# Four experts of a block beside each other in the matmul array's column quarters, and expert weights loaded as 8 KB runs per partition

## The chip, the cores and the metric

The kernel runs on one core of one Trainium2 chip. The metric is the device time of one execution in microseconds (us). The kernel before was timed three times: 866.16, 867.60 and 868.55 us, median 867.6. A separate profiled execution gives the views that are quoted below.

The engines are named as in the profile: PE is TensorE (matmuls; PEld is its load of the stationary operand), DVE is VectorE, ACT is ScalarE, POOL is GpSimd, SP is the sync engine, which here only issues transfers (SPq in the rows). DMA is the core's 16 transfer engines together.

## The reference, cut to what matters

One layer of a decoder for 256 tokens of width 1024, all in float32. A first half (normalisation, one wide input projection, a convolution branch and an attention branch, an output projection) yields a new residual `x`. The second half is a mixture of experts:

```python
h2 = rms_norm(x, norm2_g) * (1 + sc2) + sh2            # sc2, sh2: columns of c_act @ w_ada + b_ada
scores = sigmoid(h2 @ w_router)                         # 64 experts; 8 chosen per token, gates gc
g, u = split(einsum('td,edf->tef', h2, w_gu), 2)        # w_gu   (64, 1024, 512): gate and up
routed = einsum('tef,efd->td', silu(g) * u * gc, w_down) # w_down (64, 256, 1024)
out = x + g2 * (routed + shared(h2))
```

Every expert's 1024x512 gate-up matrix (2 MB) and 256x1024 down matrix (1 MB) has to be read once: 192 MB in units of 2^20 bytes, out of some 271 million bytes that the profiled execution moves.

## The kernel before, in words

**Blocks.** After routing, the kernel sorts the experts by their number of tokens and gathers the tokens of a few experts into a block of 128 rows. A block has one of four kinds: H (one expert, 128 rows), M (two experts, 96 and 32 rows), P (two experts, 64 rows each), Q (four experts, 32 rows each). There are 28 blocks: three P blocks whose experts are fixed beforehand, and then `PAT = "QPQQPQPPPMPHPMMMHPMPMPQPP"`. Numbered from 0, the Q blocks are 3, 5, 6, 8 and 25; blocks 0, 1, 2, 4, 7, 9 and so on are P; block 27, the last, is P.

**One block on PE.** `gather` picks token rows by matmuls with a 0/1 matrix (L1532) into `xt`, which holds features on partitions. `experts` then multiplies (L1785): for each of the 8 slices `k` of 128 features, and each expert of the block, the block's rows of that expert are the stationary operand and 128x512 weights stream past; the result is in one PSUM bank, each expert in its rows. The rows of an expert are also the columns of the matmul array that its product uses, so products of different experts with different rows can run beside each other. M has four such tiles of 32 rows (three of them belong to one expert), P has two of 64. `tail` applies the gate (`gate_up`: ACT L1603, DVE L1609), transposes (L1613), copies (ACT L1617), multiplies by the down weights (L1676, 2 slices `f` of features and 2 halves `h` of the output), scales (DVE L1688), splits into two parts (ACT L1745, DVE L1747), and scatters back to the tokens (PE L1699, DVE L1703).

**Parts of a Q block.** `parts("Q")` cuts the four tiles of a Q block into two pairs. The whole of gate-up is done for the first pair of experts, and then for the second pair; the down product likewise. So two of the four column quarters are in use at a time. For every other kind, `parts` is one part with all tiles.

**Weights.** All weights come through one queue that SP issues (`dma`, L269). One transfer is 1 MB: half a gate-up matrix (`("g", j, q)`, four slices of 128 features) or a whole down matrix (`("d", j, 0)`). Each goes to a slot of 8 KB per partition; a slot is free again when PE has done the last product from it (`done`), and only then does SP issue the transfer that is next in `order`. Slice `k` is features `128k` to `128k+127`, one feature per partition (`"(k p) n -> p k n"`): a partition's 8 KB in the slot are four rows of the gate-up matrix (2 KB each) or two rows of the down matrix (4 KB each), from places that are far from each other in memory.

**What sets the order of work.** The kernel is written as generators that yield costs (`yield "P", 0.87`). A planner (`Plan`) runs them at build time with estimated costs and arrival times of transfers, and thereby fixes the order of the instructions on each engine and of the transfers. At run time each engine goes through its instructions in that order and waits where it must. A different cost or a different structure anywhere gives another order, also far from the edit.

**Other places that the change touches.** `ada(i)` for i = 6 to 9 makes `sh2` and `sc2`: a product with `w_ada`, four transposes to turn the row into columns (L762), a sum over four partial results (L767), and one or two small DVE instructions. `turn` scales `x` into `xn2` (ACT L1243 or DVE L1245) and transposes it to `h2T`; the router's weights `wr` and the shared expert use the same layout of features.

Of the kernel before, what the change touches and what calls it, by code (L numbers as in the profile page):

```python
# [38 lines left out]
class Event:  # L39
    t = None  # L40
# [159 lines left out]
def tile_hybrid_block(ctx, tc, x, c, positions, w_ada, b_ada, norm1_g, w_in, conv_dw, conv_dw_b,  # L200
# [70 lines left out]
    def vec(a, n):  # L271
        return a[0].rearrange("(k p) -> k p", p=n)
# [19 lines left out]
    params += [(rbias, bcast(router_bias, NE)), (wr, w_router[0].rearrange("(k p) n -> p k n", p=P))]  # L292
# [45 lines left out]
    def parts(kd):  # L338
        ts = tiles_of[kd]
        return [ts[0:2], ts[2:4]] if kd == "Q" else [ts]  # L340

    for b, (kd, js) in enumerate(blocks):
        gs = []
        for ts in parts(kd):
            es = sorted({t[0] for t in ts})
            gs += [("g", js[e], q) for q in range(2) for e in es]
        ds = [("d", j, 0) for j in js]
        if b == len(blocks) - 1:
            ds = [("d", j, 0, cs) for cs in ENDS for j in js]
            gs = [("g", j, q, c_) for q in range(2) for c_ in range(2) for j in js]  # L350
        order += gs + ds
# [37 lines left out]
    def load(kind, i, q, cut, now):  # L389
# [19 lines left out]
        wsrc = wsrc.rearrange("(k p) n -> p k n", p=P)  # L409
# [107 lines left out]
    pcol = cst.tile([P, 96], F32, name="pcol")  # L517
    ss = cst.tile([P, 8], F32, name="ss")
# [15 lines left out]
    nc.gpsimd.dma_start(rawb[33:49], b_ada[0, 3 * D:5 * D].rearrange("(k p) -> k p", p=P))  # L534
    nc.scalar.dma_start(rawb[49:57], vec(norm2_g, P))
# [94 lines left out]
    def late_columns():  # L630
# [3 lines left out]
        nc.tensor.transpose(p[:, 0:57], rawb[0:57], ident[0:57, 0:57])  # L634
        yield AP(57)
        nc.scalar.copy(pcol[:, 32:89], p[:, 0:57])
# [92 lines left out]
    p2 = cst.tile([P, 2, K], F32, name="p2")  # L729
# [6 lines left out]
    def ada(i, pool):  # L736
# [22 lines left out]
        else:  # L759
            yield "P", 0.43  # L760
            for j in range(4):
                nc.tensor.transpose(p[:, j * P:(j + 1) * P], s[:, j * P:(j + 1) * P], ident)  # L762
            yield pl.ev("cols")
            j = 4 * (i - 6)
            o = p2.rearrange("p a k -> p (a k)")[:, j:j + 4]
            yield TS(4)
            nc.vector.tensor_reduce(o, p.rearrange("p (j g r) -> p j g r", j=4, g=4)[:, :, :, 0], axis=AX.X, op=OP.add)  # L767
            yield TS(4)
            nc.vector.tensor_tensor(o, o, pcol[:, 65 + j:69 + j], op=OP.add)
            jj = slice(j % 8, j % 8 + 4)  # L770
            yield TS(4)
            if i < 8:
                nc.vector.tensor_copy(b2c[:, jj], p2[:, 0, jj])
            else:
                nc.vector.scalar_tensor_tensor(a2c[:, jj], p2[:, 1, jj], 1.0, pcol[:, 81:89][:, jj], op0=OP.add,
                                               op1=OP.mult)
# [462 lines left out]
    def turn(t, q):  # L1239
        d = slice(q * 512, (q + 1) * 512)  # L1240
        e = yield [TS(512), AS(512)]
        if e == "A":
            nc.scalar.activation(xn2[:, t, d], x_sb[:, t, d], AF.Copy, scale=rs2[:, t, 3:4])  # L1243
        else:
            nc.vector.tensor_scalar(xn2[:, t, d], x_sb[:, t, d], rs2[:, t, 3:4], None, op0=OP.mult)  # L1245
# [354 lines left out]
    def gate_up(pg, gate, put=None):  # L1600
# [11 lines left out]
        for f in range(2):  # L1612
            nc.tensor.transpose(pg[:, f * P:(f + 1) * P], act[:, f * P:(f + 1) * P], ident)  # L1613
# [42 lines left out]
    def tail(b, pg):  # L1656
# [10 lines left out]
        for ts in parts(kd):  # L1667
            es = sorted({t[0] for t in ts})
            for e in es:
                yield pl.ev("L", "d", js[e], 0)  # L1670
                yield max(loaded["d", js[e]].at)
            for f in range(2):
                for h in range(2):
                    yield "P", 0.87
                    for e, o, m in ts:
                        nc.tensor.matmul(pd[h][o:o + m], aT[:, f, o:o + m],  # L1676
                                         loaded["d", js[e]].k[f][:, h * 512:(h + 1) * 512],
                                         start=(f == 0), stop=(f == 1))
            for e in es:
                done(("d", js[e]), 0)  # L1680
# [90 lines left out]
    def experts():  # L1771
        for b, (kd, js) in enumerate(blocks):
# [3 lines left out]
            for ts in parts(kd):  # L1776
                es = sorted({t[0] for t in ts})
                for k in range(K):
                    yield pl.ev("xt", b - b % 2, k // 2)
                    for e in es:  # L1780
                        yield pl.ev("L", "g", js[e], k // 2)
                        yield loaded["g", js[e]].at[k]
                    yield "P", 0.87
                    for e, o, m in ts:
                        nc.tensor.matmul(pg[o:o + m], info.xt[:, k, o:o + m], loaded["g", js[e]].k[k],  # L1785
                                         start=(k == 0), stop=(k == K - 1))
                    if b < 2 and k % 4 == 1:
                        for e in es:
                            if loaded["g", js[e]].off[k // 4] != LAST:
                                advance(pl.cur.ready, loaded["g", js[e]].off[k // 4])  # L1790
                    if k % 4 == 3:
                        for e in es:
                            done(("g", js[e]), k // 4)
# [147 lines left out]
```

## Time and profile before

| | |
|---|---|
| profiled execution, its own time | 866.95 us |
| its span, first to last instruction | 865.2 us |
| runs, median (lowest, highest) | 867.6 us (866.16, 868.55) |
| PE busy | 809.2 us, 94% |
| DVE, ACT, POOL busy | 464.9, 311.2, 191.6 us |
| transfers over the span | 271.03 MB, mean 313 GB/s |
| granted TensorE clock, mean | 0.982 |

Time and span are of the same execution; 1.75 us of the time lie outside the span. The first product of block 0 starts at 337 us, so about 528 of the 865 us belong to the experts. A window row of the profile gives, for a stretch of the span, the busy time of each engine with the number of its instructions in brackets, the granted clock (1.00 is full speed), the mean busy share of the 16 transfer engines (it can exceed 1 a little, where packets overlap) and the rate. A timeline row gives start, duration, engine, line, operation, operands and count. PE is counted as busy while any matmul is in flight.

### The profile page before, as it was taken

Reading aid. Unit: us, or ns where it says so; the run is one execution under the profiler, and the core shown is the slowest. Engines: PE = TensorE matmul, PEld = TensorE weight load, DVE = VectorE, ACT = ScalarE, POOL = GpSimd, SP = SyncE. Lnnn points to the kernel's source line nnn. Section 1 sums busy time; section 2 is a strip of 40 time slices with the busy share of each in tenths; the row PEclk is TensorE's granted clock in tenths of the full one; section 3 lists DMA queues with packets and bytes.
Section 4 is the critical chain, followed back from the end, with each engine's and each line's share of the span. In section 5 each row is a group of like instructions: output and inputs, shape, how many; then the busy total and the mean of one; then the engine's idle time right before and its main releaser. Section 6 shows DMA issues by size and latency. Waiting matters only on the chain.

```text
span 865.2 us, 13140 instructions
## 1 busy us (share of the span) xinstructions
PE 809.2 (94%) x4731; PEld 455.6 (53%) x4731; DVE 464.9 (54%) x1083; ACT 311.2 (36%) x682; POOL 191.6 (22%) x242
## 2 busy tenths in 40 slices
PE   3999999999858999999999999999999999999997
PEld 2897766798738776535342433434344343444233
DVE  6559999999975874206242343253433534433333
ACT  4457758667656542203020321212122121232010
POOL 3004899887514740001000000000000000000000
PEclk9999999999967999999999999999999999999999
DMA  9998678558446554999999999999999999979981
GB/s 322 366 340 288 209 253 299 184 207 273 162 152 240 187 197 176 354 389 393 355 394 397 392 397 393 392 397 393 394 392 395 374 341 362 355 278 388 398 303 50
DMA packets 127339, 271.03 MB, mean 313 GB/s; under 512 B 7085, under 2 KB 16901, under 8 KB 127272
## 3 DMA queue, kind: packets, MB, share of 16 engines
q1 hardware_dynamic: 126936, 270.00, 85.2%
q8 instruction: 37, 0.61, 0.3%
q14 instruction: 30, 0.25, 0.1%
q0 software_dynamic: 272, 0.16, 0.1%
q10 hardware_dynamic: 64, 0.02, 0.0%
HBM read 269.11 MB, written 1.05 MB: 312 GB/s over the span
## 4 chain that ended last, share of the span: by engine, by line


## 5 line engine op out<-in xcount | busy, mean ns | idle before, releaser
L1785 PE MATMUL bank<-fa 128*32 128x512 f32 (+2 forms) x1048 | 228.0, 596 | 0.1
L1703 DVE TENSOR_TENSOR fa<-fa,bank 128x512 f32<-128x512 f32 x108 | 73.3, 685 | 108.7 <-PE bank L1699 108.7
L1785 PEld LDWEIGHTS bank<-fa 128*32 128x32 f32 (+2 forms) x1048 | 63.5, 122 | 123.6 <-issue 119.2
L873 DVE SCALAR_TENSOR_TENSOR bank<-fa,tap,bank 128x256 f32<-128x256 f32 x232 | 112.9, 486 | 5.6
L1676 PE MATMUL bank<-fa 128*32 128x512 f32 (+2 forms) x496 | 111.5, 602 | 4.3 <-ACT fa L1617 4.2
L1745 ACT CAST obs<-fa 128x512 fp32r<-128x512 f32 x54 | 33.3, 619 | 150.6 <-DVE fa L1688 139.3
L1699 PE MATMUL bank<-obs,ra 128*128 128x512 f32 x216 | 78.1, 450 | 1.8 <-ACT obs L1745 0.6
L786 POOL TENSOR_TENSOR rb<-fa,rb 128x512 fp32r<-128x512 f32 x44 | 58.6, 1338 | 71.1 <-ACT rb L805 66.9
L1499 ACT ACTIVATE fa<-bank,b2c,a2c 128x256 f32<-128x256 f32 x108 | 53.2, 562 | 44.2 <-PE bank L1532 44.1
L786 POOL TENSOR_TENSOR ra<-fa,ra 128x512 fp32r<-128x512 f32 x48 | 63.9, 1339 | 21.2 <-ACT ra L805 20.6
L1699 PEld LDWEIGHTS bank<-obs,ra 128*128 128x128 f32 x216 | 33.5, 188 | 61.5 <-issue 49.7
L1532 PEld LDWEIGHTS bank<-ra 128*128 128x128 f32 x448 | 55.3, 191 | 12.3 <-issue 4.6
L1603 ACT ACTIVATE h<-bank 128x256 f32<-128x256 f32 x30 | 11.5, 383 | 135.1 <-PE bank L1785 131.1
L1532 PE MATMUL bank<-ra 128*128 128x256 f32 x448 | 59.7, 288 | 0.2 <-ACT fa L1499 0.2
L1785 PE MATMUL bank<-late_w,fa 128*64 128x512 f32 (+1 forms) x168 | 58.1, 596 | 0.0
L805 ACT CAST ra<-fa 128x512 fp32r<-128x512 f32 x76 | 46.7, 623 | 28.7 <-PE bank L822 16.3
L1609 DVE SCALAR_TENSOR_TENSOR fa<-bank,gsc,h 128x256 f32<-128x256 f32 x28 | 13.4, 482 | 75.2 <-ACT h L1603 75.2
L805 ACT CAST rb<-fa 128x512 fp32r<-128x512 f32 x68 | 42.3, 627 | 31.4 <-PE bank L822 21.8
L1676 PEld LDWEIGHTS bank<-fa 128*32 128x32 f32 (+2 forms) x496 | 26.1, 122 | 50.9 <-issue 39.7
L821 PE MATMUL bank<-ra 128*128 128x256 f32 x160 | 48.5, 303 | 3.3 <-ACT ra L1162 1.8
L1688 DVE TENSOR_TENSOR fa<-bank,fa 128x512 f32<-128x512 f32 x54 | 37.0, 686 | 25.5 <-PE bank L1676 25.5
L822 PE MATMUL bank<-ra 128*128 128x256 f32 x160 | 47.1, 295 | 0.9 <-DVE ra L1164 0.8
(380 smaller groups left out, 1375.4 us busy)
## 6 DMA issues: line engine op xcount, KB each, us to landing
fa<-in_w_exp_gu_dram SPq DMA_DIRECT2D x100, 1024.0 KB, 12.5
fa<-in_w_exp_down_dram SPq DMA_DIRECT2D x50, 1024.0 KB, 12.8
fa<-in_w_ada_dram SPq DMA_DIRECT2D x24, 1024.0 KB, 8.0
fa<-in_w_in_dram SPq DMA_DIRECT2D x22, 1024.0 KB, 7.2
late_w<-in_w_exp_gu_dram SPq DMA_DIRECT2D x19, 1024.0 KB, 14.3
late_w<-in_w_exp_down_dram SPq DMA_DIRECT2D x10, 1024.0 KB, 9.8
fa<-in_w_exp_gu_dram SPq DMA_DIRECT2D x18, 512.0 KB, 10.0
fa<-in_w_in_dram SPq DMA_DIRECT2D x12, 512.0 KB, 8.7
```

The lines of the kernel that those rows point to most:

```text
L786: (nc.gpsimd if e == "G" else nc.vector).tensor_tensor(hl[:, 1], w.k[k], hl[:, 0].bitcast(F32), op=OP.subtract)
L805: nc.scalar.copy(hl[:, 0], w.k[k])
L821: nc.tensor.matmul(o, hl[:, 0, mm], src_t[:, k, 0], start=(k == 0 and m % 2 == 0), stop=False)
L822: nc.tensor.matmul(o, hl[:, 0, mm], src_t[:, k, 1], start=False, stop=False)
L873: nc.vector.scalar_tensor_tensor(cv[:, m] if j == TAPS - 1 else acc, u_sb[:, m, j:j + T], tap[:, m, j:j + 1], acc, op0=OP.mult, op1=OP.add)
L1499: nc.scalar.activation(xt[:, k, 0:ns], p3[:, f2, 0:ns], AF.Identity, bias=b2c[:, k:k + 1], scale=a2c[:, k:k + 1])
L1532: nc.tensor.matmul(p3[:, f2, 0:ns], xr[:, a, t, (f + f2) * P:(f + f2 + 1) * P], pm_[:, t, 0:ns], start=(f2 + t + a == 0), stop=(f2 + t + a ...
L1676: nc.tensor.matmul(pd[h][o:o + m], aT[:, f, o:o + m], loaded["d", js[e]].k[f][:, h * 512:(h + 1) * 512], start=(f == 0), stop=(f == 1))
L1688: nc.vector.tensor_tensor(o32, pd[h], g2b[:, h * 512:(h + 1) * 512], op=OP.mult)
L1699: nc.tensor.matmul(p, info.pT[:, t * P:(t + 1) * P], obs[h][a], start=(a == 0), stop=(a == 1))
L1703: nc.vector.tensor_tensor(x_sb[:, t, d], x_sb[:, t, d], p, op=OP.add)
L1785: nc.tensor.matmul(pg[o:o + m], info.xt[:, k, o:o + m], loaded["g", js[e]].k[k], start=(k == 0), stop=(k == K - 1))
```

## The change

Three things are done.

1. `parts` is gone: the products of a Q block run over all four experts for each slice `k` (gate-up) and for each `f`, `h` (down). The weights of a Q block are loaded in the order: first halves of the four gate-up matrices, second halves, four down matrices. The number of matmuls stays the same.
2. A partition now takes neighbouring features: the expert and shared matrices are read with `"(p k) n -> p k n"`, so slice `k` is features `8p + k` (gate-up) or `2p + k` (down), and the 8 KB that a partition takes in one transfer are one run in memory. For the pieces of the last block's gate-up matrices it is 4 KB; for the column pieces of its down matrices the runs stay as they were.
3. Everything that meets those features is permuted to fit: `turn` reads `x` with a stride of eight elements, the transposes after the gate read `act` with a stride of two, the router's weights are read with the new layout, and `ada(6..9)` makes its columns by eight matmuls with one output column each (stationary operand: every eighth column of the row, 64 of them) in place of four transposes and a sum. The planner's cost of that step is 1.0 in place of 0.43. The biases and `norm2_g` for it are now loaded column-wise, both on POOL's queue, in runs of 32 bytes.

```diff
-    def parts(kd):
-        ts = tiles_of[kd]
-        return [ts[0:2], ts[2:4]] if kd == "Q" else [ts]
-
     for b, (kd, js) in enumerate(blocks):
-        gs = []
-        for ts in parts(kd):
-            es = sorted({t[0] for t in ts})
-            gs += [("g", js[e], q) for q in range(2) for e in es]
+        gs = [("g", j, q) for q in range(2) for j in js]
         ds = [("d", j, 0) for j in js]
...
-        wsrc = wsrc.rearrange("(k p) n -> p k n", p=P)
+        wsrc = wsrc.rearrange("(p k) n -> p k n" if kind in ("g", "d", "sg", "sd") else "(k p) n -> p k n", p=P)
...
-    nc.gpsimd.dma_start(rawb[33:49], b_ada[0, 3 * D:5 * D].rearrange("(k p) -> k p", p=P))
-    nc.scalar.dma_start(rawb[49:57], vec(norm2_g, P))
+    nc.gpsimd.dma_start(c2[:, 0:2], b_ada[0, 3 * D:5 * D].rearrange("(a p k) -> p a k", a=2, k=K))
+    nc.gpsimd.dma_start(c2[:, 2], norm2_g[0].rearrange("(p k) -> p k", k=K))
...
-            yield "P", 0.43
-            for j in range(4):
-                nc.tensor.transpose(p[:, j * P:(j + 1) * P], s[:, j * P:(j + 1) * P], ident)
+            h = slice(64 * (i % 2), 64 * (i % 2) + 64)
+            sv = s.rearrange("p (c k) -> p k c", k=K)
+            yield "P", 1.0
+            for k in range(K):
+                nc.tensor.matmul(p[h, k:k + 1], sv[:, k], sel4[:, 0:1], start=True, stop=True)
...
+        o = xn2[:, t, d].rearrange("p (k c) -> p k c", k=4)
+        xk = x_sb[:, t].rearrange("p (c k) -> p k c", k=K)[:, 4 * q:4 * q + 4]
...
-            nc.vector.tensor_scalar(xn2[:, t, d], x_sb[:, t, d], rs2[:, t, 3:4], None, op0=OP.mult)
+            nc.vector.tensor_scalar(o, xk, rs2[:, t, 3:4], None, op0=OP.mult)
...
-            nc.tensor.transpose(pg[:, f * P:(f + 1) * P], act[:, f * P:(f + 1) * P], ident)
+            nc.tensor.transpose(pg[:, f * P:(f + 1) * P], act.rearrange("s (c f) -> s f c", f=2)[:, f], ident)
...
-        for ts in parts(kd):
-            es = sorted({t[0] for t in ts})
-            for e in es:
-                yield pl.ev("L", "d", js[e], 0)
-                yield max(loaded["d", js[e]].at)
-            for f in range(2):
-                for h in range(2):
-                    yield "P", 0.87
-                    for e, o, m in ts:
+        for j in js:
+            yield pl.ev("L", "d", j, 0)
+            yield max(loaded["d", j].at)
+        for f in range(2):
+            for h in range(2):
+                yield "P", 0.87
+                for e, o, m in tiles_of[kd]:
...
-            for ts in parts(kd):
-                es = sorted({t[0] for t in ts})
-                for k in range(K):
-                    yield pl.ev("xt", b - b % 2, k // 2)
-                    for e in es:
-                        yield pl.ev("L", "g", js[e], k // 2)
-                        yield loaded["g", js[e]].at[k]
-                    yield "P", 0.87
-                    for e, o, m in ts:
+            for k in range(K):
+                yield pl.ev("xt", b - b % 2, k // 2)
+                for j in js:
+                    yield pl.ev("L", "g", j, k // 2)
+                    yield loaded["g", j].at[k]
+                yield "P", 0.87
+                for e, o, m in tiles_of[kd]:
```

How this moves instructions is seen on PE in block 25, the last Q block. The rows are line, operation, operands, size of the output and how many follow each other; L1785 is gate-up, L1699 the scatter of an earlier block, L1578 and L1581 small products for a later block. Before, gate-up of the first pair is the two rows with x8, that of the second pair the row with x16:

```order
L1785 MATMUL bank_79<-fa 32x512 x8
L1578 MATMUL bank_74<-ra 128x4 x2
L1581 LDWEIGHTS permb
L1581 MATMUL bank_74<-rtb,permb 64x256
L1581 LDWEIGHTS permb
L1581 MATMUL bank_74<-rtb,permb 64x256
L1699 MATMUL bank_78<-obs,ra 128x512 x2
L1699 MATMUL bank_80<-obs,ra 128x512 x2
L1785 MATMUL bank_79<-fa 32x512 x8
L1699 MATMUL bank_77<-obs,ra 128x512 x2
L1699 MATMUL bank_76<-obs,ra 128x512 x2
L1785 MATMUL bank_79<-fa 32x512 x16
```

In the changed kernel (gate-up is its L1773, the scatter L1689) the same 32 matmuls stand in groups of four, one per expert, which is seen where one of the four experts' weights lie in another buffer (`late_w`):

```order
L1773 MATMUL bank_80<-fa 32x512 x16
L1689 MATMUL bank_78<-obs,ra 128x512 x2
L1773 MATMUL bank_80<-fa 32x512 x2
L1773 MATMUL bank_80<-late_w,fa 32x512
L1773 MATMUL bank_80<-fa 32x512 x3
L1773 MATMUL bank_80<-late_w,fa 32x512
L1773 MATMUL bank_80<-fa 32x512 x3
L1773 MATMUL bank_80<-late_w,fa 32x512
L1773 MATMUL bank_80<-fa 32x512 x3
L1773 MATMUL bank_80<-late_w,fa 32x512
L1773 MATMUL bank_80<-fa 32x512
L1605 MATMUL bank_80<-ident,fa 128x128 x2
```

What moved: the first 16 matmuls (slices 0 to 3) now need the first halves of all four experts, and the next 16 the second halves.

On SP, at the same block's transfers (`TENSOR_LOAD` reads the number of the next expert), the queue before takes two experts' first and second halves, and then the next expert:

```order
L398 TENSOR_LOAD ids
L398 ISA x2
L269 ISA
L269 DMA fa<-in_w_exp_gu_dram 128x4x512
L269 ISA
L269 DMA fa<-in_w_exp_gu_dram 128x4x512
L269 ISA
L269 DMA fa<-in_w_exp_gu_dram 128x4x512
L398 TENSOR_LOAD ids
L398 ISA x2
L269 ISA
L269 DMA fa<-in_w_exp_gu_dram 128x4x512
```

and in the changed kernel first halves of expert after expert:

```order
L391 TENSOR_LOAD ids
L391 ISA x2
L269 ISA
L269 DMA fa<-in_w_exp_gu_dram 128x2048
L391 TENSOR_LOAD ids
L391 ISA x2
L269 ISA
L269 DMA fa<-in_w_exp_gu_dram 128x2048
L391 TENSOR_LOAD ids
L391 ISA x2
L269 ISA
L269 DMA fa<-in_w_exp_gu_dram 128x2048
```

What moved: the order of halves, and the form of a transfer, 128 runs of 2048 floats in place of 128 times four runs of 512. The number of transfers and their bytes are the same. In the first half of the program the order of attention and projection work on PE is also another one from the first changed `ada` step on, because the planner was given another cost there.

More of the change, by code (lines that the diff above doesn't have):

```diff
@@ L633, in late_columns @@
         yield "P", 0.1
-        nc.tensor.transpose(p[:, 0:57], rawb[0:57], ident[0:57, 0:57])
-        yield AP(57)
-        nc.scalar.copy(pcol[:, 32:89], p[:, 0:57])
+        nc.tensor.transpose(p[:, 0:33], rawb[0:33], ident[0:33, 0:33])
+        yield AP(33)
+        nc.scalar.copy(pcol[:, 32:65], p[:, 0:33])
         yield "P", 0.3
@@ L726, in angles @@
         pl.set("lam")
-    p2 = cst.tile([P, 2, K], F32, name="p2")
+    p2 = cst.tile([P, K], F32, name="p2")
     a2c = cst.tile([P, K], F32, name="a2c")
@@ L1666, in tail @@
         pd = yield Get("bank", 2)
[L1667 to L1680 removed]
+        for j in js:
[5 more added lines that the diff above has]
+                for e, o, m in tiles_of[kd]:
+                    nc.tensor.matmul(pd[h][o:o + m], aT[:, f, o:o + m],
+                                     loaded["d", js[e]].k[f][:, h * 512:(h + 1) * 512],
+                                     start=(f == 0), stop=(f == 1))
+        for j in js:
+            done(("d", j), 0)
         pl.put("aT", aT)
@@ L1775, in experts @@
             pg = yield Get("bank")
-            for ts in parts(kd):
-                es = sorted({t[0] for t in ts})
-                for k in range(K):
-                    yield pl.ev("xt", b - b % 2, k // 2)
-                    for e in es:
-                        yield pl.ev("L", "g", js[e], k // 2)
-                        yield loaded["g", js[e]].at[k]
-                    yield "P", 0.87
-                    for e, o, m in ts:
[L1785 to L1793, printed above, removed]
+            for k in range(K):
+                yield pl.ev("xt", b - b % 2, k // 2)
+                for j in js:
+                    yield pl.ev("L", "g", j, k // 2)
+                    yield loaded["g", j].at[k]
+                yield "P", 0.87
+                for e, o, m in tiles_of[kd]:
+                    nc.tensor.matmul(pg[o:o + m], info.xt[:, k, o:o + m], loaded["g", js[e]].k[k],
+                                     start=(k == 0), stop=(k == K - 1))
+                if b < 2 and k % 4 == 1:
+                    for j in js:
+                        if loaded["g", j].off[k // 4] != LAST:
+                            advance(pl.cur.ready, loaded["g", j].off[k // 4])
+                if k % 4 == 3:
+                    for j in js:
+                        done(("g", j), k // 4)
             info.users[0] -= 1
@@ L1905, in tile_hybrid_block @@
                 for f in range(2):
-                    nc.tensor.transpose(B[2 + t][:, f * P:(f + 1) * P], act[:, f * P:(f + 1) * P], ident)
+                    nc.tensor.transpose(B[2 + t][:, f * P:(f + 1) * P], act.rearrange("s (c f) -> s f c", f=2)[:, f],
+                                        ident)
                 nc.scalar.copy(aT.rearrange("p f s -> p (f s)"), B[2 + t][:, 0:T])
```

23 lines of the change are left out of this document (9 added, 14 removed).

## Prediction

> **What bounds the kernel now.** I read the page's slices first, then windows over the five stretches of the expert stage, then PE's and SP's timelines for where a block starts and when its weights are asked for.
>
> ```profile
> PE   3999999999858999999999999999999999999997
> DMA  9998678558446554999999999999999999979981
> 337.00:377.10 40.10, 39.86 (x202) 18.56 (x201) 7.52 (x24) 9.48 (x20) 0.00 (x0) 1.00 0.87 317
> 377.10:538.90 161.80, 158.75 (x788) 62.63 (x787) 57.96 (x131) 30.88 (x65) 5.55 (x4) 1.00 1.03 390
> 538.90:804.30 265.40, 258.21 (x1496) 109.63 (x1495) 104.69 (x230) 61.72 (x127) 0.00 (x0) 1.00 1.00 372
> 804.30:828.50 24.20, 22.71 (x111) 6.83 (x110) 7.19 (x14) 1.90 (x4) 0.00 (x0) 1.00 1.04 393
> ```
>
> From 337 us on, PE is in flight 97 to 99% of the time (the first number after each length), and the transfer engines are full as well (share 1.03, 390 GB/s, between 377.1 and 538.9). Both look like the bound. Which one is it? The next rows are the starts of blocks 3, 9, 25 and 27 on PE and issues on SP.
>
> ```profile
> 372.12 0.99 SPq L269 DMA_DIRECT2D fa<-in_w_exp_gu_dram  x2
> 375.55 6.17 SPq L269 DMA_DIRECT2D fa<-in_w_exp_down_dram  x4
> 377.10 2.34 PE L1785 MATMUL bank<-fa 128*32 128x512 f32 x10
> 477.00 21.45 SPq L269 DMA_DIRECT2D fa<-in_w_exp_gu_dram  x8
> 509.13 1.05 PE L1785 MATMUL bank<-fa 128*32 128x512 f32 x4
> 538.92 0.64 PE L1785 MATMUL bank<-late_w,fa 128*64 128x512 f32 x1
> 804.30 1.05 PE L1785 MATMUL bank<-fa 128*32 128x512 f32 x4
> 842.27 3.60 PE L1785 MATMUL bank<-fa 128*64 128x512 f32 x16
> 852.83 0.64 PE L1718 MATMUL bank<-fa 128*64 128x512 f32 x1
> fa<-in_w_exp_gu_dram SPq DMA_DIRECT2D x100, 1024.0 KB, 12.5
> ```
>
> Block 8, a Q block, starts at 509.1 us. Its eight gate-up transfers are issued from 477.00 to 498.45 and land 12.5 us after issue in the median, so each is there well before PE comes to it. PE never waits for weights; a transfer waits for a slot that PE has to empty. PE sets the pace, and the queue has nothing in reserve: with PE faster, it is next.
>
> **Part 1, the Q blocks on PE.** Gate-up in windows around blocks 5 (Q), 7 (P), 12 (M) and 25 (Q); the first number after the length is PE's busy time in L1785 alone. Then one down product of a P block.
>
> ```profile
> 420.50:456.50 36.00, 14.43 (x64) 3.64 (x66) 1.00 1.04 394
> 493.80:509.10 15.30, 7.28 (x32) 2.09 (x32) 1.00 1.05 387
> 589.00:605.40 16.40, 7.28 (x64) 1.87 (x65) 1.00 1.04 394
> 804.30:828.50 24.20, 14.31 (x64) 3.46 (x64) 1.00 1.04 393
> 838.78 3.65 PE L1676 MATMUL bank<-fa 128*64 128x512 f32 x16
> ```
>
> The M row is what a Q block will be: 64 records of 32 columns in 7.28 us, four tiles side by side, as fast as the 32 records of a P block. A Q block's 64 records take 14.3 to 14.4 now. The change therefore saves 7.1 us of gate-up per Q block, and in the down product one of two passes of 3.65 us: 10.8 us a block, 54 us for five. M streams one matrix three times where Q streams four, but each matmul is a record with its own stream, so I take M's row for Q.
>
> The Trainium skill, "TensorE: Matmul & The Clock Gate", section "Measured speedup vs the span model", speaks against this: three column tiles gave 2.38 times there, not 3. By it a pass of four would take 7.28/0.79 = 9.2 us, and the sum would be some 3 us higher, for block 25 alone, since the others end in a wait for weights anyway. The trace's M row does not show that loss.
>
> **Part 2, the transfers.** The rate of the queue by the run length, in stretches with one kind of weights: 1 KB runs (`w_ada` pieces at the start), 4 KB (down, twice), 2 KB (gate-up, twice). The last two numbers are the busy share and GB/s.
>
> ```profile
> 5.20:10.80 5.60, 0.00 (x0) 0.00 (x0) 4.18 (x40) 1.81 (x5) 1.00 (x2) 1.00 1.06 355
> 380.00:389.80 9.80, 9.80 (x58) 2.85 (x54) 0.00 (x0) 0.00 (x0) 0.00 (x0) 1.00 1.02 411
> 507.20:517.20 10.00, 10.00 (x56) 4.75 (x56) 4.34 (x10) 4.17 (x8) 0.00 (x0) 1.00 1.04 405
> 493.50:506.90 13.40, 13.03 (x58) 4.15 (x59) 5.21 (x10) 1.99 (x4) 0.00 (x0) 1.00 1.05 387
> 565.80:576.00 10.20, 10.20 (x44) 3.37 (x43) 5.18 (x11) 1.57 (x3) 0.00 (x0) 1.00 1.04 391
> ```
>
> A transfer of 2^20 bytes takes 1.0486 MB over the rate: 2.95 us at 1 KB, 2.70 at 2 KB, 2.55 to 2.59 at 4 KB. Each doubling saves about half of what the last did, 0.25 and then 0.13. No row has 8 KB; one more halving gives 2.50. Bounds: 2.57, if 4 KB is already as good as it gets, and 2.42, if the next step saved as much as the last. I take 2.49.
>
> **The sum.** First the blocks from 3 to 8 (Q P Q Q P Q). PE needs 161.8 - 4 x 10.8 = 118.6 us for them. The rate of 411 from 380.0 on is that of block 3's down matrices, so its gate-up weights were in by about 380; earlier transfers wait for slots that blocks 0 to 2 empty, which the change leaves alone, so I take 378. From there to the first halves of block 9 there are 4 + 6 + 12 + 12 + 6 + 12 + 2 = 54 transfers, 54 x 2.49 = 134.5 us, the end at 512.5. That is later than PE would be (377.1 + 118.6 = 495.7), so weights set the pace here, and PE waits 17 us. Block 9 starts at 512.5 in place of 538.9: **-26.4 us**. Slots do not hold the queue back there: a Q block's products now empty four slots at a time in a quarter of the time that the queue needs to fill them.
>
> Blocks 9 to 24 hold eight P, six M and two H: 90 transfers, 224 us, against 265.4 us of PE that the change does not touch. PE sets the pace again, the lead grows, the gain is kept. Block 25 is a Q block with the lead restored: **-10.8**. After it come 12 transfers (30 us) beside 842.3 - 804.3 - 10.8 = 27 us of PE; the queue is some 10 us ahead in the rows above, which covers it: **+0.5**.
>
> The first half pays for the layout.
>
> ```profile
> L762 PE MATMUL bank<-ident,fa 128*128 128x128 f32 x16 | 2.5, 276 | 0.8 <-ACT fa L748 0.8
> L1578 PE MATMUL bank<-ra 128*128 128x4 f32 x42 | 7.6, 250 | 0.0
> 111.00:178.00 67.00, 62.79 (x360) 1.00 0.72 252
> L1245 DVE TENSOR_SCALAR fa<-fa,rs 128x512 f32<-128x512 f32 x2 | 1.0, 477 | 0.7 <-POOL rs L1235 0.7
> L1613 PE MATMUL bank<-ident,fa 128*128 128x128 f32 x60 | 12.3, 289 | 5.8 <-DVE fa L1609 5.8
> L1703 DVE TENSOR_TENSOR fa<-fa,bank 128x512 f32<-128x512 f32 x108 | 73.3, 685 | 108.7 <-PE bank L1699 108.7
> ```
>
> `ada(6..9)`: 16 transposes (2.5 us) go, 32 matmuls with one column come, at 7.6/42 = 0.18 us each by the nearest row (four columns) 5.8 us: +3.3 on PE, which is 94% busy there and has other work to put beside a wait; I take half, +1.6. The two strided DVE scalings of `turn` may rise from 0.48 to the 0.69 us of a DVE instruction on 512 elements with two inputs: +0.4, on the chain to the router. The strided `act` transposes, the router's layout and the two small loads on POOL's queue I put at nothing: the first are as many instructions as before, the others end long before use; were the strided transposes half again as slow, 60 of 0.29 us would cost 4 us in part. **+2.0**, with 0 and 8 as the ends.
>
> Together 865.2 - 26.4 - 10.8 + 0.5 + 2.0 = 830.5 us of span, with the 1.75 outside it 832.2, against 866.95 of this execution. The median of the runs is 0.65 higher, so 832.9: I say **832**. With 2.42 and 2.57 the first term is -30 and -22; with the first half's ends the likeliest case spans 824 to 842.
>
> **Rivals.**
>
> *Long runs gain nothing.* If the rate is set by bytes and not by runs, 54 transfers take 54 x 2.66 = 143.6 us, block 9 starts at 521.6, and the time is 841. Against it: the three rising rates above. Chance 0.12.
>
> *The weights do not bind, PE's saving comes in full.* Then 54 + 3 us less the 2.5 paid: 815. It needs 54 transfers in 118 us, 2.2 each, 480 GB/s, which no row comes near, or an earlier start of the queue. 0.06.
>
> *The clock drops where PE now waits.* The rows: windows with PE's busy time and the granted clock.
>
> ```profile
> 238.60:242.00 3.40, 1.91 (x10) 1.00 1.05 393
> 242.00:245.50 3.50, 1.69 (x6) 0.66 1.05 387
> 295.00:300.00 5.00, 3.83 (x16) 1.00 0.64 211
> 300.00:305.00 5.00, 3.53 (x16) 1.00 0.58 210
> ```
>
> At about half busy the clock fell, at 70 to 77% it stayed. PE would be busy 118.6 of 134.5 us, 88%, but in bursts with gaps of up to 6 us between a block's halves. If a third of the work ran at half clock, PE would need 158 us there, and the gain of blocks 3 to 8 shrinks from 26 to 4: about 854. A few slow bursts only use up PE's own waiting. The skill's page "TensorE: Matmul & The Clock Gate", section "HAM oscillation — how this bites in real kernels", describes just such bursts that start cold after each wait for a transfer; the rows agree that waiting lowers the clock. 0.09.
>
> *The new order of the first half costs.* The planner's changed cost moves attention and projections; 5 to 15 us lost there give 837 to 847 (and as much could be won). 0.07.
>
> *Slower than before.* Reading 8 KB at a time, the 16 engines take places 64 KB apart and each fills one partition for long; if they then meet in the same memory or port, the queue slows. After block 3's gate-up there are 166 transfers, and from the last block's down product to the end are 865.2 - 852.8 = 12.4 us: the time is worse than before from (865.2 - 12.4 - 378)/166 = 2.86 us a transfer on, 367 GB/s, below all but the 1 KB row. 0.04.
>
> *The four tiles do not overlap,* no gain on PE: 867 to 870. The M row is against it. 0.01.
>
> **How the numbers follow.** The forecast's case has 0.61. 820 to 848 holds it, the first rival, and most of the order's and the clock's cases, and leaves about 2 in 10 out. A measurement of this kernel tells a difference of 0.3%, 2.6 us, from none; the runs above spread by that. Faster by more: 0.93; the slow side of the clock's and the order's cases and the missing overlap leave 0.02 within it; slower 0.05.
>
> **What would show it.** Right: L1785 in a Q block 7.3 us; the rate between blocks 3 and 8 about 421 GB/s, with PE waiting for transfers some 17 us there and hardly at all after block 11; block 9 near 512 plus what the first half shifted; block 25 13 us long. Wrong: a rate at or below 411 (the second part fails), PE busy without gaps between 380 and 510 (weights do not bind), a granted clock under 1 there, or block 0 not starting within 335 to 342.

## The result, and the profile after

The changed kernel takes 841.04 us (median of four runs, 838.2 to 842.8), the kernel before, run on the same chip, 867.88 us. The ratio is 0.969, with a 95% interval of 0.966 to 0.972: about 27 us, where 35 were forecast. The profiled execution took 842.05 us, its span is 840.3 us.

First the page's slices of the changed kernel, one digit for each of 40 equal stretches of 21 us; the last row is in GB/s.

```profile
PE   3999999899987999999998988999999999999897
PEclk9999999699997999999999999999999999999999
DMA  9998666545564684799999999999999989969792
GB/s 314 364 361 289 241 226 241 200 158 195 200 213 157 207 324 164 285 348 423 422 418 422 421 421 420 421 421 420 422 420 422 417 328 383 340 269 422 296 404 82
```

From the nineteenth slice (378 us) on, the queue runs at 417 to 423 GB/s for fourteen slices without a dent, and after that with dents: there it waits for slots. PE has its dents ("8") where the queue has none. Next the windows of the changed kernel over the stages that the prediction used (length, then PE, PEld, DVE, ACT, POOL busy, granted clock, share, GB/s). Block 0 starts at 339.0 us, block 3 at 379.2, block 9 at 516.7, block 25 at 789.0, block 26 at 803.0.

```profile
339.00:379.20 40.20, 39.95 (x205) 18.70 (x206) 7.56 (x24) 9.52 (x20) 0.00 (x0) 1.00 0.86 322
379.20:516.70 137.50, 127.82 (x787) 58.90 (x786) 55.84 (x128) 30.16 (x63) 5.56 (x4) 0.98 1.01 421
516.70:789.00 272.30, 264.08 (x1511) 114.48 (x1513) 110.76 (x241) 64.01 (x130) 0.00 (x0) 1.00 0.96 390
789.00:803.00 14.00, 12.44 (x101) 3.44 (x100) 2.91 (x5) 0.76 (x2) 0.00 (x0) 0.96 0.72 283
803.00:840.30 37.30, 31.09 (x140) 12.07 (x136) 15.13 (x27) 3.99 (x8) 0.00 (x0) 0.97 0.58 219
```

Blocks 3 to 8 fell from 161.8 to 137.5 us. Blocks 9 to 24 rose from 265.4 to 272.3, and block 25 fell from 24.2 to 14.0. The last two belong together, since ten instructions, mostly scatter pairs of earlier blocks, now stand ahead of block 25's first product. So the fair windows are blocks 9 to 23 and blocks 24 with 25, first of the kernel before, then of the changed one.

```profile
538.90:785.30 246.40, 239.67 (x1403) 100.89 (x1402) 97.94 (x215) 55.67 (x114) 0.00 (x0) 1.00 0.99 371
785.30:828.50 43.20, 41.25 (x208) 15.57 (x204) 13.95 (x30) 7.94 (x16) 0.00 (x0) 1.00 1.04 395
```

```profile
516.70:764.90 248.20, 241.99 (x1403) 103.61 (x1402) 99.72 (x217) 56.82 (x116) 0.00 (x0) 1.00 0.96 390
764.90:803.00 38.10, 34.53 (x208) 14.31 (x204) 13.95 (x30) 7.95 (x16) 0.00 (x0) 0.96 0.88 355
```

Blocks 24 and 25 together fell by 5.1 us, not by 10.8. Set side by side, from the two spans:

| stretch | forecast | measured |
|---|---|---|
| up to block 0 | +2.0 | +2.0 |
| block 0 to block 9 | -26.4 | -24.2 |
| blocks 9 to 23 | 0 | +1.8 |
| blocks 24 and 25 | -10.8 | -5.1 |
| blocks 26 and 27 | +0.5 | +0.6 |
| span | -34.7 | -24.9 |

The time of 841 is also just what the first rival, "long runs gain nothing", gave. The time alone would have confirmed a mechanism that the 421 GB/s refute. What the experiments had to tell apart is the bound in each stretch, and where the missing 10 us are.

### The profile page after: what moved, and what is told of

Read it like the earlier page. It is cut to its first block, busy times and chain, and to the rows that moved or that the text cites. A ratio compares the mean times of both kernels' runs of the same rounds, so it can differ in the third digit from the quotient of the medians.

```text
span 840.3 us, 13229 instructions
## 1 busy us (share of the span) xinstructions
PE 784.8 (93%) x4779; PEld 463.0 (55%) x4779; DVE 461.1 (55%) x1074; ACT 316.1 (38%) x685; POOL 193.1 (23%) x246
## 4 chain that ended last, share of the span: by engine, by line
## 5 line engine op out<-in xcount | busy, mean ns | idle before, releaser
L1773 PE MATMUL bank<-fa 128*32 128x512 f32 (+2 forms) x1024 | 207.1, 599 | 1.6 <-DMA fa<-in_w_exp_gu_dram 1.4
L1773 PEld LDWEIGHTS bank<-fa 128*32 128x32 f32 (+2 forms) x1024 | 59.6, 123 | 105.3 <-issue 95.7
L1666 PE MATMUL bank<-fa 128*32 128x512 f32 (+2 forms) x520 | 102.0, 604 | 5.7 <-ACT fa L1609 5.1
L1689 PE MATMUL bank<-obs,ra 128*128 128x512 f32 x216 | 77.1, 451 | 2.8 <-DVE obs L1737 1.4
L1773 PE MATMUL bank<-late_w,fa 128*32 128x512 f32 (+1 forms) x192 | 76.6, 596 | 0.0
L776 POOL TENSOR_TENSOR rb<-fa,rb 128x512 fp32r<-128x512 f32 x46 | 60.3, 1317 | 63.5 <-ACT rb L795 60.6
L776 POOL TENSOR_TENSOR ra<-fa,ra 128x512 fp32r<-128x512 f32 x48 | 63.8, 1334 | 24.2 <-ACT ra L795 22.9
L1689 PEld LDWEIGHTS bank<-obs,ra 128*128 128x128 f32 x216 | 34.8, 191 | 58.4 <-issue 45.8
L1666 PEld LDWEIGHTS bank<-fa 128*32 128x32 f32 (+2 forms) x520 | 24.6, 122 | 49.3 <-issue 34.9
```

Source lines behind the costliest of these rows:

```text
L776: (nc.gpsimd if e == "G" else nc.vector).tensor_tensor(hl[:, 1], w.k[k], hl[:, 0].bitcast(F32), op=OP.subtract)
L1666: nc.tensor.matmul(pd[h][o:o + m], aT[:, f, o:o + m], loaded["d", js[e]].k[f][:, h * 512:(h + 1) * 512], start=(f == 0), stop=(f == 1))
L1689: nc.tensor.matmul(p, info.pT[:, t * P:(t + 1) * P], obs[h][a], start=(a == 0), stop=(a == 1))
```

## Experiments

Each kernel's time is a median; ratios are against the kernel before on the same chip, with the 95% interval. Starts of blocks are the first gate-up product of a block on PE. The kernel before had medians from 866.7 to 868.2 us on the chips used, so a difference of 1 us between two kernels that ran on different chips says little.

### The two parts, each alone

The first kernel has the merged parts with the old layout, for the weights and for everything that meets their features. As against the changed kernel:

```diff
-        wsrc = wsrc.rearrange("(p k) n -> p k n" if kind in ("g", "d", "sg", "sd") else "(k p) n -> p k n", p=P)
+        wsrc = wsrc.rearrange("(k p) n -> p k n", p=P)
```

The second has the 8 KB layout, with `parts` back in the weights' order, the gate-up and the down products:

```diff
+    def parts(kd):
+        ts = tiles_of[kd]
+        return [ts[0:2], ts[2:4]] if kd == "Q" else [ts]
```

> The change's part 1 alone: four experts of a Q block side by side, matrices read in the old layout (2 KB and 4 KB runs). Theory, weights set the pace from block 3 to block 9 and the run length sets the queue's rate: 54 transfers at 2.66 us are 143.6 us in place of 134.7, block 9 starts near 523 (before 538.9, changed kernel 516.7), the rate there stays near 393 GB/s with a share above 1, the first half is as before, time 847 to 850. Rival, run length is worth nothing and all the gain is PE's: the rate is the changed kernel's or the wait is as short, time 838 to 841.

> Part 2 alone: the new layout with runs of 8 KB and everything that is permuted for it, Q blocks still in two pairs. Theory, PE sets the pace as in the kernel before: the rate where the queue is busy is 421 GB/s, weights are further ahead of PE, nothing is gained, the first half costs about 2 us, time 868 to 871. Rival, the queue was the bound in part of the expert stage before: 855 to 862.

Part 1 alone took 849.3 us (0.979, 0.977 to 0.981), part 2 alone 872.4 us (1.006, 1.004 to 1.008). The windows from block 3 to block 9, part 1 alone first, then part 2 alone:

```profile
379.10:525.80 146.70, 130.56 (x787) 58.42 (x786) 55.81 (x128) 30.16 (x63) 5.56 (x4) 0.99 1.04 394
```

```profile
379.40:541.60 162.20, 159.19 (x790) 63.49 (x789) 58.14 (x131) 30.88 (x65) 5.55 (x4) 1.00 0.99 407
```

With part 1 alone the queue is as full as in the kernel before (share 1.04), at 394 GB/s, and block 9 starts at 525.8 in place of 516.7: 9.1 us, as 54 transfers at 2.66 in place of 2.49 us make it. In the trace's packets block 3's last gate-up transfer lands at 382.0 and block 9's first halves at 525.7, 2.66 us a transfer; in the changed kernel at 381.2 and 515.9, 2.49. With part 2 alone PE is in flight for 159.2 of 162.2 us, the queue has time to spare (0.99), and nothing is gained. Part 1 is worth 17 us by itself and 27 with part 2, and part 2 by itself is 5.7 us worse than nothing: the weights set the pace between blocks 3 and 8 only once PE is faster. The theory held for the time and the rate of part 1 alone, although block 9 started 2.8 us after the 523 that it named; part 2 alone came out 1.4 us slower than it said. Of the 5.4 us between its profile and the first one of the kernel before, 2.3 lie ahead of block 0 and 1.9 in block 25.

### More work on PE, early and late

If weights set the pace in blocks 3 to 8 and PE in blocks 9 to 24, then the same added work is nearly free in the one place and costs its full length in the other. Both kernels repeat the first gate-up step three times, in four blocks; planner and order are untouched. The blocks are 3, 5, 6 and 8 in the first kernel and 12, 16, 18 and 21 in the second.

```diff
+PAD_BLOCKS = (3, 5, 6, 8)
...
+                for _ in range(3 if k == 0 and b in PAD_BLOCKS else 0):
+                    for e, o, m in tiles_of[kd]:
+                        nc.tensor.matmul(pg[o:o + m], info.xt[:, 0, o:o + m], loaded["g", js[e]].k[0],
+                                         start=True, stop=True)
```

> The changed kernel with its order untouched, and three more copies of the first gate-up step (slice 0, all four tiles) in each of the Q blocks 3, 5, 6 and 8: 4 x 3 x 0.91 = 10.9 us more work on PE, no other work. Theory (between blocks 3 and 8 the weights set the pace, and PE has waits to put the work in): block 9 starts at 516.5 to 519.5 as against 516.7, the time is 841 to 845. Rival (PE sets the pace there too, and the gaps are only the order's): block 9 starts near 527, the time is 851 to 853.

> The same 10.9 us of added products, in the M blocks 12, 16, 18 and 21 of the changed kernel, where the weights lie 7 to 31 us ahead of PE. Theory (PE sets the pace there): the time is 850 to 853, block 25 starts 10 to 11 us later, near 799.5. Rival (what lies between PE's products there, waits for DVE and ACT or the queue, sets the pace and takes the work in): under 847.

Early: 844.4 us (840.9 to 845.3), 3.4 more than the changed kernel. In the profile block 2 starts 148.3 us ahead of block 9, against 146.2: 2.1 us for 10.9 us of work. Late: 852.4 us (849.4 to 855.8), 11.3 more; from block 11 to the end 300.8 us against 289.1. Both times are as the theory said; block 9 of the early kernel started at 515.3, 1.2 us ahead of the stated range, because block 0 started 3.5 us earlier in that profile. The 11.7 us hold some clock, though. These are the windows from the start of block 11 to the start of block 24, of the changed kernel and of the late one:

```profile
551.20:764.90 213.70, 208.18 (x1246) 88.54 (x1242) 86.08 (x187) 49.03 (x100) 0.00 (x0) 1.00 0.95 385
```

```profile
551.90:775.90 224.00, 218.49 (x1344) 91.74 (x1340) 86.12 (x187) 48.99 (x100) 0.00 (x0) 1.00 0.92 366
```

At full clock in both, the 10.9 us of work cost 10.3. Blocks 24 and 25 took another 1.6 us more (39.7 against 38.1), where the half clock lasted 6.8 us in place of 3.4. The early kernel's window from block 3 to block 9 holds a surprise:

```profile
378.20:515.30 137.10, 129.18 (x862) 58.51 (x854) 55.12 (x126) 30.05 (x63) 5.56 (x4) 1.00 1.00 413
```

There are 75 more records on PE than in the changed kernel's window, and PE is in flight only 1.4 us longer, in part because the granted clock is 1.00 where it was 0.98. These are windows of the changed kernel, 3.4 us each, in pairs:

```profile
445.40:448.80 3.40, 1.69 (x9) 1.06 (x9) 2.62 (x8) 0.37 (x1) 0.00 (x0) 1.00 1.01 422
448.80:452.20 3.40, 3.40 (x18) 3.40 (x18) 0.00 (x0) 1.45 (x3) 0.00 (x0) 0.50 1.01 419
506.80:510.20 3.40, 1.58 (x7) 0.48 (x7) 0.45 (x1) 0.37 (x1) 0.00 (x0) 1.00 1.02 424
510.20:513.60 3.40, 2.81 (x10) 0.42 (x14) 0.00 (x0) 0.00 (x0) 0.00 (x0) 0.50 1.01 419
783.30:786.70 3.40, 1.85 (x10) 1.03 (x8) 3.01 (x6) 1.24 (x2) 0.00 (x0) 1.00 0.78 234
786.70:790.10 3.40, 3.40 (x15) 1.60 (x18) 2.38 (x6) 0.00 (x0) 0.00 (x0) 0.50 0.99 417
```

Each time a window in which PE was in flight for about half (1.58 to 1.85 of 3.40 us) is followed by one at half clock. In the early kernel the two windows between blocks 3 and 8 are gone. The share in flight alone is no rule, though. This window of the changed kernel starts four window lengths after the last of these, and full clock follows it:

```profile
796.90:800.30 3.40, 1.84 (x18) 0.60 (x14) 0.48 (x1) 0.76 (x2) 0.00 (x0) 1.00 1.01 426
800.30:803.70 3.40, 3.40 (x32) 0.99 (x26) 1.19 (x2) 0.57 (x1) 0.00 (x0) 1.00 1.01 429
```

The window from 465.9 us is a second such case, also with 1.84 us, and part 1 alone has one with 1.68 us from 507.0. What sets them apart stays open. The Trainium skill, "TensorE: Matmul & The Clock Gate", section "HAM oscillation — how this bites in real kernels", gives the rule that PE should have no idle gaps of more than about 3.4 us; here the longest single gap ahead of such a window was 1.71 us, so this trace shows the clock falling without such a gap.

### The down products in pairs

The changed kernel with the old down products, in two pairs per Q block; gate-up and runs as changed.

```diff
+        for ts in ([tl[0:2], tl[2:4]] if kd == "Q" else [tl]):
...
+            for f in range(2):
+                for h in range(2):
+                    yield "P", 0.87
+                    for e, o, m in ts:
```

> The changed kernel with the down products of a Q block in two pairs again; gate-up by four, 8 KB runs as they are. Theory (the two pairs of before already overlapped in part when they ran back to back: 5.3 us for both in block 25, not 2 x 3.65): in block 25 the down products take 5.3 to 5.4 us in place of 3.64, blocks 3 to 8 hide theirs behind the weights, the time is 841 to 844. Rival (two full passes, as the prediction summed them): 7.3 us in block 25 and 844 to 846.

847.0 us (844.9 to 848.0): the theory was right on block 25 and too low on the time. The windows show L1669 alone, this kernel's down products, for block 25:

```profile
791.20:809.10 17.90, 5.38 (x32) 1.42 (x32) 0.96 0.78 306
```

5.38 us for the two pairs, not 7.3. The kernel before had the same; its windows for L1676 in block 25, and a piece of PE's timeline in it:

```profile
804.30:828.50 24.20, 5.31 (x32) 1.42 (x32) 1.00 1.04 393
```

```profile
824.50 0.59 PE L1676 MATMUL bank<-fa 128*32 128x512 f32 x1
824.51 0.59 PE L1676 MATMUL bank<-late_w,fa 128*32 128x512 f32 x1
824.93 0.59 PE L1676 MATMUL bank<-fa 128*32 128x512 f32 x1
824.94 0.62 PE L1676 MATMUL bank<-late_w,fa 128*32 128x512 f32 x2
824.95 1.00 PE L1676 MATMUL bank<-fa 128*32 128x512 f32 x2
825.37 0.62 PE L1676 MATMUL bank<-late_w,fa 128*32 128x512 f32 x2
```

Up to 824.9 two products start every 0.43 us; from then on four do. The second pair's products, which use the other two column quarters, start while the first pair is still under way. Two pairs back to back had half of the overlap already, and 1.75 us was to be gained in block 25, not 3.65. In blocks 3 and 5 of the kernel with pairs, scatter products stand between the groups of down products, and there these were in flight for 7.6 and 6.8 us, about two full passes: the overlap came where the pairs stood back to back. L1666 over block 25 in the changed kernel:

```profile
789.00:803.00 14.00, 3.56 (x32) 0.94 (x32) 0.96 0.72 283
```

What was not expected is a loss ahead of block 9, which starts 182.0 us after block 0, against 177.7. Between 432 and 464 us the queue stood at 0.96 and 389 GB/s in that kernel, where it ran at 420 to 421 in the changed one; the packets show one landing there 4.1 us after the last, where 2.5 is the rule. The down products of blocks 3 and 5 are 3 to 4 us longer each and give their slots back later; that this is what held the queue is likely, but it was not tested by itself.

### The order of blocks

Two patterns. The first spreads the Q blocks evenly and begins with M, P and H; the second exchanges just two blocks of the changed kernel, 8 and 17.

```diff
-PAT = "QPQQPQPPPMPHPMMMHPMPMPQPP"
+PAT = "MPHPQMPPQMPHQMPPQMPPQMPPP"
```

```diff
-PAT = "QPQQPQPPPMPHPMMMHPMPMPQPP"
+PAT = "QPQQPMPPPMPHPMQMHPMPMPQPP"
```

> The changed kernel with the blocks in another order, PAT MPHPQMPPQMPHQMPPQMPPQMPPP: the five Q blocks, which need 12 transfers (30 us) beside some 18 us of PE, stand between blocks that need more PE than transfers. Theory, PE's wait of some 17 us in blocks 3 to 8 is only a matter of their standing together: it goes, PE sets the pace to the end, time 815 to 825; the floor is the queue, 381 + 166 x 2.49 + 12 = 806 in span. Rival, PE in blocks 3 to 8 waits for something else (the in-order chain through ACT and DVE, slots): the wait moves with the Q blocks, 835 to 843.

> The changed kernel with two blocks exchanged in the pattern: block 8 is an M block and block 17 a Q block. Theory (weights set the pace up to block 8, and from block 16 on the queue stands with all slots full, 16 to 30 us ahead, so that it has time to give): block 8 takes about 15.5 us in place of 22.6, block 9 starts near 509.5 and no longer waits; block 17 is 1 to 2 us longer; the time is 833 to 837. Rival (the six transfers that are put off are missed later, or the order by the planner takes the gain back): 840 to 844.

The even spread took 836.3 us (0.965, 0.963 to 0.967): under 5 us gained, the rival's range. Its windows over blocks 3 to 6, 7 to 22 and 23 to 26:

```profile
377.40:451.70 74.30, 71.15 (x361) 34.10 (x360) 29.12 (x68) 15.29 (x33) 5.56 (x4) 0.98 0.76 303
451.70:745.80 294.10, 280.94 (x1735) 124.13 (x1733) 123.63 (x271) 70.09 (x144) 0.00 (x0) 0.99 1.01 416
745.80:809.40 63.60, 60.05 (x362) 24.13 (x363) 21.95 (x43) 10.65 (x22) 0.00 (x0) 1.00 1.01 419
```

Without a Q block before 450 us the slots fill up and the queue idles a quarter of that time; from then on it is full to the end, and the weights of blocks 24 to 26 land 0 to 3 us before their use. What the queue did not move early it lacked late; this is a reading of the windows, and the next kernel was built on it.

The reading gave the exchange of two blocks: one Q block less where the queue is behind (block 8), one more where it stood with full slots (block 17; the changed kernel's weights there land 16 to 31 us ahead of use). It took 830.0 us (828.7 to 830.8; 0.956, 0.953 to 0.958), 11 us under the changed kernel and 3 us under what the theory gave. It is the best kernel of this study, 38 us under the one before. Its windows over blocks 3 to 8, 9 to 24, and 24 with 25:

```profile
378.50:506.10 127.60, 122.69 (x788) 57.95 (x787) 55.91 (x128) 30.11 (x63) 5.55 (x4) 0.99 1.01 421
506.10:778.10 272.00, 262.32 (x1511) 112.57 (x1509) 110.13 (x242) 63.96 (x130) 0.00 (x0) 1.00 0.98 405
...
755.00:791.60 36.60, 33.03 (x209) 13.77 (x205) 13.82 (x30) 7.94 (x16) 0.00 (x0) 1.00 0.95 383
```

Block 9 starts 9.9 us earlier after block 3 than in the changed kernel (127.6 against 137.5), and the stretch to block 25 does not grow (272.0 against 272.3). Among PE's waits from block 3 to block 25 no transfer is left: the six transfers that were put off are not missed. The last row, blocks 24 and 25, is the changed kernel's work at full clock; against 38.1 us there it says that the half clock at 786.7 cost about 1.5.

### A planner that knows the new rate

The planner still counts 2.92 us for a transfer. Here it counts 2.49 for the experts' weights; nothing else is changed, but the order moves with it.

```diff
-        size = 2.92 / max(cuts, 1)
+        mb = 2.49 if kind in ("g", "d") else 2.92
+        size = mb / max(cuts, 1)
```

> The changed kernel, with the planner told that a 1 MB transfer of expert weights takes 2.49 us (measured) in place of 2.92: only the order of instructions and of transfers changes. Theory, the 5 us that blocks 24 and 25 lost against the sum come from an order that was planned for late weights (scatter products of earlier blocks stand together in front of block 25 and wait for ACT and DVE): blocks 24 and 25 together go from 38.1 to 33 to 35 us, time 834 to 838. Rival, the clock's half-speed window at 786.7 is the cause and comes wherever a Q block ends: 840 to 843.

842.9 us (839.9 to 844.8), no gain; the theory fell on the time. Blocks 24 and 25 took 32.3 us, but block 27 with the end took 38.9 in place of 23.5: work changed places.

### The first half, and the strided reads

Two small terms of the prediction had not been tested so far: the 2.0 us of the first half, and the strided transposes that were put at nothing. The first kernel is the one before, once more. The second is the kernel with blocks 8 and 17 exchanged, with the permutation done where VectorE writes the gated product:

```diff
+        ao = act.rearrange("s (f c) -> s c f", f=2)
+        up, sv = (a.rearrange("s (c f) -> s c f", f=2) for a in (pg[:, 256:512], sg))
-            nc.vector.scalar_tensor_tensor(act, pg[:, 256:512], gate, sg, op0=OP.mult, op1=OP.mult)
+            nc.vector.scalar_tensor_tensor(ao, up, gate, sv, op0=OP.mult, op1=OP.mult)
-            nc.tensor.transpose(pg[:, f * P:(f + 1) * P], act.rearrange("s (c f) -> s f c", f=2)[:, f], ident)
+            nc.tensor.transpose(pg[:, f * P:(f + 1) * P], act[:, f * P:(f + 1) * P], ident)
```

> The kernel before once more, for a second profile of its first half, which the kernel with part 1 alone shares to the instruction. Theory (the first half varies by 1 to 2 us from run to run, and the 2.0 us that the changed kernel's block 0 started later are within that): block 0 starts at 337 to 339.5 us. Rival (it is steady to a few tenths, and 339.0 in the changed kernel is the price of the new layout): 336.8 to 337.2.

> The kernel with blocks 8 and 17 exchanged, and the 8 KB layout's permutation of the gated product done where VectorE writes it (in the order f, then c) in place of where TensorE loads it for the transposes, which then read dense rows. Order as it was. Theory (a weight load of a strided operand costs 197 ns against 141, and it stands on PE's path): the 60 loads take 141 ns each again, the two strided VectorE operands cost little (484 ns become under 600), the time falls by 1 to 3 us, to 827 to 829. Rival (the loads lie beside other products, or VectorE pays as much as PE saves): 829.5 to 832.

The kernel before took 867.7 us, in its one run. Its block 0 started at 337.7 us this time (337.0 in the first profile), and at 339.0 in the kernel with part 1 alone, which has the same instructions in the same order up to there. In nine profiles of kernels with the new layout it started between 335.5 and 339.3. The first half varies by as much as the term, so the term is not resolved.

The second kernel took 831.4 us (830.7 to 833.9; 0.957, 0.955 to 0.960), 1.4 more than without the edit. That is not clear of the noise, but nothing was gained; its theory fell. The groups of the transposes' weight loads and of the gate's multiplication (duration in ns, lowest, median, highest), before the edit and after it:

```profile
L1605 PEld LDWEIGHTS bank<-ident,fa x60: 194/198/222, 357.0 to 815.2; 128*128 128x128 f32 x60
L1601 DVE SCALAR_TENSOR_TENSOR fa<-bank,gsc,h x28: 476/484/486, 356.0 to 814.5; 128x256 f32<-128x256 f32 x28
```

```profile
L1607 PEld LDWEIGHTS bank<-ident,fa x60: 137/141/143, 356.8 to 818.4; 128*128 128x128 f32 x60
L1603 DVE SCALAR_TENSOR_TENSOR fa<-bank,gsc,h x28: 651/660/685, 355.7 to 817.6; 128x256 f32<-128x256 f32 x28
```

TensorE saves 2 x 57 ns a block, VectorE pays 176 ns on the chain that PE waits for. In the profiles blocks 9 to 23, at full clock in both, took 250.1 us with the edit and 248.9 without. So reading with the stride in the transpose is the cheaper place. Next to dense rows that stride costs little here: with part 2 alone blocks 9 to 23 took 246.7 us, in the kernel before 246.4.

## Why the prediction was right, and where it was wrong

**What bounds what: right.** PE set the pace before, if not quite as fully as the prediction read it: its fourth row, block 25, has PE in flight 94% of the time and not 97 to 99. With PE faster the weights set the pace from block 3 to block 8, and PE again after block 9. The two padded kernels show it directly, 2.1 and 10.3 us for the same 10.9 us of work, and part 1 alone shows the price of a transfer in the first stretch.

**Gate-up in four tiles: right.** L1773 alone in the changed kernel, around blocks 6, 8 and 25:

```profile
457.60:472.80 15.20, 7.26 (x64) 1.85 (x60) 1.00 1.01 420
494.10:506.60 12.50, 9.33 (x64) 2.09 (x64) 1.00 1.01 422
789.00:803.00 14.00, 7.79 (x64) 1.89 (x64) 0.96 0.72 283
```

At full clock and without a wait 7.26 us, as the M row said. The 9.2 us that the prediction worked out from the Trainium skill, "TensorE: Matmul & The Clock Gate", section "Measured speedup vs the span model", do not appear there. Block 8's 9.33 us come near them in number only: its products ran at full clock, but a few at a time with 1.43 us of waiting for a transfer between them, so that each piece stayed in flight by itself. Block 25's 7.79 us hold 1.1 us at half clock at their start.

**The rate: right,** and it was the boldest number, carried over from 1, 2 and 4 KB to 8 KB: 2.49 us a transfer, 421 GB/s. The first rival falls with it.

**Blocks 3 to 8: 2.2 us too much gained.** The step that failed is the start of the count: I took 378 us for the landing of block 3's gate-up weights in the kernel before. The packets have it at 379.8 there, and at 381.2 in the changed kernel: 1.2 us after 378 and the 2.0 us of the first half. PE started 0.8 us after the last landing, and the 54 transfers took 0.2 us more than the sum. My reason was the rate of 411 from 380.0 on, and that only says that the down matrices were under way by then. The 17 us that PE was to wait did not show as waits for transfers. These are all of PE's waits for transfers between blocks 3 and 9, with the two larger ones for DVE (us in total, times, longest):

```profile
PE bank L1605 <- DVE fa L1601: 2.9, 4, 1.1
PE bank L1524 <- DVE ra L1516: 1.7, 1, 1.7
PE bank L1773 <- DMA fa<-in_w_exp_gu_dram: 1.4, 1, 1.4
...
PE bank L1666 <- DMA late_w<-in_w_exp_down_dram: 0.8, 1, 0.8
PE bank L1666 <- DMA fa<-in_w_exp_down_dram: 0.6, 1, 0.6
```

2.8 us, and all idle time of PE in that stretch is 9.7. PE was in flight for 127.8 us there, not 118.6: the down products fell from 39.3 to 29.7 us, 2.4 a Q block in place of the 3.65 of the sum, block 8's gate-up came in pieces, and part of the work ran at half clock. The rival on the clock (0.09) happened in small, although the share in flight, by which the prediction told when the clock falls, does not decide it by itself. It cost little in that stretch, because the queue set the end of it anyway.

**Blocks 24 and 25: 5.7 us too much gained.** This is the largest error, and the step is the sum for block 25, "one of two passes of 3.65 us". The window of L1676 over block 25 would have shown 5.31 us for both passes before anything was run; I multiplied a row by a count instead. That is 1.9 us. PE's idle time in the two blocks rose from 1.95 to 3.57 us, 1.6 more. The half clock cost 1.5, by the exchanged kernel. Some 0.7 remain unexplained. The new waits are in PE's timeline ahead of block 25:

```profile
784.53 0.50 PE L1689 MATMUL bank<-obs,ra 128*128 128x512 f32 x1 [0.50 <-ACT obs L1735]
786.09 0.50 PE L1689 MATMUL bank<-obs,ra 128*128 128x512 f32 x1 [1.05 <-DVE obs L1737]
...
788.96 1.08 PE L1773 MATMUL bank<-fa 128*32 128x512 f32 x4
```

Scatter products that stood between the gate-up products of block 25 now stand ahead of them and wait one by one for ACT and DVE. That the long gate-up of before had been the cover for those waits is read from the two orders and was not tested by itself; the prediction did not name it.

**Blocks 9 to 23: put at nothing, cost 1.8 us.** Blocks 9 and 10 took 34.5 us in place of 33.0, all others are within 0.2 us. In the exchanged kernel they took 33.4, so most of it goes with what lies just before block 9, the tight weights or the half clock. The kernel with added work early has no half clock there, and its blocks 9 and 10 took 35.0. So the half clock is not needed for it; that the tight weights are the cause was not tested by itself.

**The end and the first half.** +0.6 for +0.5. The +2.0 of the first half was met by the number, but what two kernels with the same instructions show lies 2 us apart, so this is luck and no proof.

So the range held the time, and the likeliest value was 9 us too low. In the profiled execution, which is 1 us slower than the median, 9.8 us of span were missing: 5.7 in blocks 24 and 25, 2.2 in blocks 3 to 8 (1.2 of them an anchor that was not looked up), 1.8 in blocks 9 to 23, and 0.1 at the end. Two small sums of the prediction do not come out either: the low end of its likeliest case adds up to 826 and not 824, and 54 + 3 - 2.5 us off the time give 813 and not 815. Neither moves its range.

## What to carry to other kernels

What products cost is read from the window of their line over the stage, not from a count times one row: products of neighbouring groups may overlap already, and then merging them gains less. When PE gets faster in one stretch only, the order of the blocks has to follow: here moving one weight-heavy block to where the queue stood full was worth 11 us, two fifths of what the change itself brought, for an exchange of two letters. A time that fits a rival's number is no evidence for it; the rate, the window and a padded kernel told the two apart.

## What had not been expected of the hardware

- The granted clock halved for 3.4 us after a 3.4 us window with PE in flight 1.58 to 1.85 us, although no gap was longer than 1.71 us; other windows with 1.84 us in flight were followed by full clock. With 2.7 us of idle products per block, two of the half-clock windows did not come.
- Products in different column quarters start beside each other even when they belong to different groups in the queue, if these stand back to back: 32 products of two pairs took 5.31 us where two passes of 3.65 would be 7.3.
- A weight load with a stride of two elements took 198 ns in place of 141, and a VectorE instruction on 256 elements with strided operands 660 ns in place of 484.
- The queue's packets filled the 16 engines to 1.04 at runs of 2 and 4 KB and 394 GB/s, and to 1.01 at 8 KB runs and 421 GB/s.
